# A two-layer hybrid mixer block: narrow matmuls grouped by shape, and the order of all instructions made anew

## The chip, the cores and the metric

The kernel runs on one core of a Trainium2 chip. Its metric is the device time of one execution in microseconds (us), from which the median of several executions is taken. Five engines work side by side, each through its own queue in order: TensorE (PE in the profile; its weight loads are PEld), VectorE (DVE), ScalarE (ACT), GpSimd (POOL) and SyncE (SP), which issues the DMAs here.

## The reference

Two layers over a stream x (512 tokens, 1024 channels), and in the first layer also over a context stream (256 tokens). Each layer scales and shifts the stream by vectors made from a condition (the modulation), projects it, mixes it in four ways, projects back, and applies a gated feed-forward block, with a layer norm after each half. Cut to what the change touches:

```python
def modulation(cond, w, b):                   # for two conditions, 6 x 1024 columns
    m = (jax.nn.silu(cond) @ w + b)[..., None, :]
    return jnp.split(m, 6, axis=-1)

# rwkv_prep, both directions d: two low-rank products (LoRA) of 64 columns each
logw  = -jax.nn.softplus(-(w0[d] + jnp.tanh(dw) @ w2[d])) - 0.5
decay = jnp.exp(-jnp.exp(logw)); a = jax.nn.sigmoid(a0[d] + da @ a2[d])

def step(S, inp):                             # rwkv_scan: token after token, 4 heads of 64
    s_kk = jnp.einsum('bhvk,bhk->bhv', S, -kk_t)
    S = S * w_t + s_kk[..., None] * (kk_t * a_t) + v_t[..., None] * k_t
    return S, jnp.einsum('bhvk,bhk->bhv', S, r_t)
```

The context is scanned first and hands its states to x. The other mixers (pooling, a gated MLP over chunks of 128 tokens, a Fourier mixer) and the feed-forward block are dense work beside the scan.

## The kernel before

Most of the arithmetic is dense: the projections and the feed-forward block multiply in three passes of fp32r (`mm3`: high by high, high by low, low by high), with 128 rows and 128 columns of the array in use and 512 or 256 tokens moving. Weights come as raw tiles of 128x1024 (512 KB, three buffers); ACT rounds them to a high part and DVE subtracts to get the low part (`wsplit`).

Between these stand matmuls that fill only a part of the array:

- `mod` (L671) makes two of the six modulation vectors. For each of 8 blocks of rows and each of two vectors it loads one raw tile and runs two matmuls of 32 columns and 512 moving elements (`ps<-raw,sc`). A raw tile fills two of the four groups of 32 columns, the next tile the other two. There are 5 such calls, 80 raw tiles in all; the first modulation is made in `start` in another layout, which already uses all four column groups with 256 elements.
- `group` (L1088) prepares 4 chunks of 64 tokens for one pair of heads, in both directions, and is called 12 times. It makes the LoRA products, the high part on 128 rows (`lh`), the low part on the 64 rows of its direction (`ll`); then, for each head, four matmuls with weights from `BK` on 64 rows, and four transposes of `BK` on 64 rows.
- `inverse` (L1188), once a group, inverts eight triangular 64x64 blocks. The diagonal blocks of 16 are solved by substitution on DVE: 15 shuffles of rows (`NR<-Nc`), then 15 pairs of a product (`Rt`) and a sum (`Rc`). Blocks of 32 and 64 follow from matmuls of 32x32 in two stages, 96 of them.
- `scan` (L1248) takes four steps. A step has four or five places where both directions d of both heads e each need one small matmul: 64 columns on 128 rows (`ps<-page` 64x64), or 64 on 64 (`ps<-rhs,page`). The heads lie in different halves of the array's columns.

The code does not issue instructions in the order in which it is written. `Program` keeps each as an `Op` with an estimated cost; `latest` gives it a latest start, `LEAD` (L255) moves each labelled part by a number of nanoseconds, and `schedule` (L353) places instructions one by one by that priority, if buffers suffice. A TensorE instruction of another kind than the last costs `SWITCH` there, and kinds are only fp32r or not. Each matmul is its own `Op`, so that the three of an `mm3` or the four of a scan place can be torn apart. Scans run beside dense work: `main` merges the two parts with `both`.

Of the kernel before, what the change touches and what calls it, by code (L numbers as in the profile page):

```python
# [32 lines left out]
# packed constants  # L33
C_B64 = 0
C_MG = 128
C_M0, C_E0, C_E1, C_D16 = 640, 704, 736, 768
C_SCAN = 784
C_EDGE = 1040
C_RW = 1072
C_N = 1074  # L40
# [7 lines left out]
P_N = 72  # L48

# [3 lines left out]
def part(f):  # L53
    """A method whose instructions are moved together in time."""

    def g(self, *a, **k):
        p = self.nc
        up, p.lab = p.lab, (*p.lab, f.__name__, *(getattr(x, "name", x) for x in a if isinstance(x, (int, Stream))))
        r = f(self, *a, **k)
        p.lab = up  # L60
        return r

    return g


class Op:
    """One instruction, held back until its place is known."""

    def __init__(self, i, eng, meth, args, kw, lab):
        self.i, self.eng, self.meth, self.args, self.kw, self.lab = i, eng, meth, args, kw, lab  # L70
# [4 lines left out]
        self.outs, self.ins = outs, ins  # L75
        self.dma = meth == "dma_start"
        self.table = ACT_SET.get(kw.get("func")) if eng == "scalar" else None
        self.price()

    def price(self):  # L80
        """Estimated time on its engine and until others see its result, in ns."""
        size = lambda a: math.prod(c for _, c in list(a.ap)[1:])
        n, k = size(self.outs[0]), self.kw
        ps = any(a.space == PSUM for a in self.outs + self.ins)
        ptr = sum(isinstance(k.get(x), bass.AP) for x in ("scale", "bias", "scalar1", "scalar2", "scalar"))
        if self.dma:
            self.cost, self.bytes = 60.0, 4 * n * self.outs[0].partition_size()
        elif self.eng == "tensor":
            w = self.args[1]
            m, kp = size(w), w.partition_size()  # L90
            self.table = 1 + (w.dtype == F32R)
            self.cols = n * kp / 128 * (1 if w.dtype == F32R else 2 if self.meth == "transpose" else 4)
            if w.dtype == F32R:
                self.cost = (n if n >= 256 else 4 * max(n, m)) / 2.4 + 2.5
            elif self.meth == "transpose":
                self.cost = 2 * kp / 2.4 + 2.5
            elif m > 64:
                self.cost = 4 * max(n, m) / 2.4 + 5
            else:
                self.cost = n / 1.2 + 30 if m > 32 else n / 2.4 + 26 if kp > 32 else 35.0  # L100
        elif self.eng == "vector":
            if self.meth in ("tensor_reduce", "bn_stats"):
                n = size(self.ins[0])
            elif self.meth == "bn_aggr":
                n = 8
            elif self.meth == "reciprocal":
                n *= 6
            elif self.meth in ("tensor_copy", "tensor_scalar", "memset") and not ps:
                n /= 2
            self.cost = 69 + n / 0.96 + 61 * ptr  # L110
        elif self.eng == "scalar":
            self.cost = (51 if ps else 93) + n / 1.2 + 93 * ptr
        elif k.get("op") == ALU.pow:
            self.cost = 300 + 165 * n
        else:
            self.cost = 110 + n * {"tensor_tensor": 2.24, "tensor_copy": 3.4, "tensor_scalar": 5.6}.get(self.meth, 1)


class Program:
    """Takes the place of nc: keeps the instructions of the kernel as a list."""  # L120
# [8 lines left out]
    def __init__(self, nc):  # L129
        self.nc, self.ops, self.lab = nc, [], ()  # L130
        for e in ENGINES:
            setattr(self, e, Program.Engine(self, e))

    def add(self, eng, meth, args, kw):
        self.ops.append(Op(len(self.ops), eng, meth, args, kw, self.lab))

    def both(self, a, b):
        """Two independent parts, merged by their progress."""
# [16 lines left out]
class Tiles:  # L155
    """Stands in for the tile pools: gives tiles their memory when their first instruction is placed."""
# [36 lines left out]
def region(a, cache={}):  # L193
    """Partitions and the set of free elements (as bits) that an access covers."""
# [13 lines left out]
def analyse(ops):  # L208
    """What each instruction has to come after, and the tiles it touches.

    A matmul that starts a sum also acts on the other sums in the same rows of its bank."""
    live = {}
    for o in ops:
        o.preds, o.succ, o.tiles = set(), [], []
        new = []
        for w, aps in ((True, o.outs), (False, o.ins)):
            for a in aps:
                nm = a.name
                if a.space == DRAM:
                    if not nm.startswith("keep"):  # L220
                        continue
                    p0, p1, m = 0, 1, 1
                else:
                    if nm not in o.tiles:
                        o.tiles.append(nm)
                    p0, p1, m = region(a)
                acc = o.kw.get("start") if w and o.eng == "tensor" else None
                for j, jw, q0, q1, jm, je, jacc in live.get(nm, ()):
                    if j in o.preds or (not w and not jw and not (a.space == PSUM and je != o.eng)):
                        continue  # L230
                    if (a.space == PSUM and je != o.eng) or (p0 < q1 and q0 < p1 and (
# [1507 lines left out]
```

## Time and profile before

| | |
|---|---|
| time, median of 3 runs | 1966.04 us (1961.61 to 1971.19) |
| span of the profiled execution, first to last instruction | 1969.1 us |
| PE busy | 1851.2 us, 94% of the span |
| PE weight loads busy | 1399.8 us, 71% |
| DVE busy | 1330.0 us, 68% |
| ACT, POOL busy | 728.1 us, 589.6 us (37%, 30%) |
| moved by DMA | 233.56 MB, 119 GB/s over the span |

The profiled execution has no time of its own beside its span; the span lies inside the range of the three timed runs. An fp32 matmul leaves two records in the profile, an fp32r matmul or a transpose one, so that x8 in a row of `ps<-page 128x64` is four matmuls. A record's end is modelled and reaches into the next, so rows of neighbours overlap. Nearly all instructions carry line L491, the line that emits them; they are told apart by the names of their tiles.

### The profile page before, as it was taken

How to read it: one execution, taken by the hardware profiler on the slowest of the kernel's cores; microseconds unless marked ns; L12 is line 12 of the kernel's file. 1: busy time of each engine (PE TensorE's matmuls, PEld its weight loads, DVE VectorE, ACT ScalarE, POOL GpSimd, SP SyncE). 2: the span in 40 equal slices, each digit the busy share in tenths (PEclk: the TensorE clock that was granted, in tenths of full speed). 3: DMA queues.
4: the chain of work that ended last, by engine and by line, in shares of the span. 5: the costliest groups of instructions: out<-in, count | busy, mean ns of one | idle time of the engine just before them, and what ended most of it. 6: DMA issues, size and time to landing. Idle time of an engine off the chain costs nothing. (4 is left out here: it accounts for less than half of the span.)

```text
span 1969.1 us, 32607 instructions
## 1 busy us (share of the span) xinstructions
PE 1851.2 (94%) x12400; PEld 1399.8 (71%) x12400; DVE 1330.0 (68%) x3047; ACT 728.1 (37%) x1445; POOL 589.6 (30%) x651
## 2 busy tenths in 40 slices
PE   7999899899989999899999999999989999999996
PEld 4886655587867668778777777767545677788875
DVE  3596968887998688734745478786895953443446
ACT  2573643444643334422322232544432232222220
POOL 3132443331342334600112114222553361100015
PEclk9998899899999999999999998988889999999998
DMA  8532147453534651333222232211454323323241
GB/s 295 182 109 80 65 153 224 149 166 130 176 125 155 199 170 59 106 97 97 86 93 79 83 100 92 81 55 31 135 182 153 113 83 94 97 86 107 86 128 43
DMA packets 86221, 233.56 MB, mean 119 GB/s; under 512 B 9008, under 2 KB 10416, under 8 KB 86064
## 3 DMA queue, kind: packets, MB, share of 16 engines
q1 hardware_dynamic: 86064, 231.48, 36.5%
q8 instruction: 97, 1.59, 0.3%
q14 instruction: 60, 0.49, 0.1%
HBM read 225.15 MB, written 6.29 MB: 118 GB/s over the span
## 5 line engine op out<-in xcount | busy, mean ns | idle before, releaser
L491 PE MATMUL ps<-page,w 128*128 128x512 f32 (+1 forms) x4512 | 957.5, 362 | 40.1 <-DVE w L491 26.4
L491 PEld LDWEIGHTS ps<-page,w 128*128 128x128 f32 x4512 | 742.2, 193 | 199.6 <-DVE w L491 45.2
L491 DVE TENSOR_TENSOR w<-raw,w 128x512 fp32r<-128x512 f32 (+1 forms) x526 | 407.2, 791 | 387.6 <-PE ps L491 312.6
L491 POOL TENSOR_TENSOR page<-page 128x512 f32<-128x512 f32 (+6 forms) x266 | 345.2, 1308 | 765.7 <-DVE page L491 616.1
L491 ACT ACTIVATE w<-raw 128x512 fp32r<-128x512 f32 (+1 forms) x526 | 314.5, 624 | 590.4 <-PE ps L491 458.3
L491 PE MATMUL ps<-w,page 128*128 128x512 f32 (+1 forms) x1704 | 413.2, 380 | 10.6 <-DVE w L491 6.0
L491 PEld LDWEIGHTS ps<-w,page 128*128 128x128 f32 x1704 | 295.0, 190 | 81.1 <-DVE w L491 10.4
L491 PE MATMUL ps<-page 128*64 128x64 f32 (+1 forms) x1832 | 219.2, 284 | 8.0 <-DVE page L491 3.7
L491 PEld LDWEIGHTS ps<-page 128*64 128x64 f32 (+1 forms) x1832 | 157.2, 157 | 87.1 <-issue 29.1
L491 ACT ACTIVATE page<-ps 128x512 f32<-128x512 f32 (+5 forms) x271 | 109.8, 421 | 218.9 <-PE ps L491 210.4
L491 DVE TENSOR_TENSOR page<-ps,page 128x512 f32<-128x512 f32 x210 | 143.0, 684 | 52.7 <-PE ps L491 42.4
L491 PE MATMUL ps<-raw,sc 128*32 128x512 f32 (+1 forms) x448 | 106.3, 574 | 12.8 <-DMA raw<-in_w_mod_dram 6.4
L491 POOL TENSOR_TENSOR page<-half,page 128x256 fp32r<-128x256 f32 (+2 forms) x72 | 61.1, 852 | 163.3 <-DVE page L491 107.2
L491 POOL TENSOR_TENSOR Sd<-page,pc 64x128 f32<-64x128 f32 x88 | 44.7, 508 | 154.1 <-DVE page L491 139.6
L491 ACT ACT_TABLE_LOAD x58 | 74.4, 1283 | 10.9 <-DVE half L491 7.1
L491 DVE TENSOR_TENSOR page<-ps,cst 64x256 f32<-64x256 f32 (+1 forms) x136 | 66.7, 498 | 13.3 <-PE ps L491 11.0
L491 POOL TENSOR_TENSOR page<-page,half 64x256 f32<-64x256 f32 (+1 forms) x54 | 45.8, 849 | 97.6 <-DVE half L491 52.4
L491 DVE TENSOR_TENSOR Rt<-Rc,NR 128x16 f32<-128x16 f32 (+4 forms) x180 | 73.6, 409 | 1.4
L491 DVE STREAM_SHUFFLE NR<-Nc 128x120 f32<-128x120 f32 (+4 forms) x180 | 67.6, 560 | 0.0
L491 PE MATMUL ps<-idn,page 128*128 128x128 f32 (+1 forms) x276 | 53.6, 305 | 6.9 <-ACT page L491 2.4
L491 DVE SCALAR_TENSOR_TENSOR page<-ps,pc,Sd 64x64 f32<-64x64 f32 x176 | 43.4, 280 | 21.4 <-PE ps L491 19.0
L491 PEld LDWEIGHTS ps<-page,BK 64*128 64x128 f32 x384 | 42.8, 198 | 18.5 <-issue 12.9
(123 smaller groups left out, 1439.7 us busy)
## 6 DMA issues: line engine op xcount, KB each, us to landing
raw<-in_w_dram SPq DMA_DIRECT2D x196, 512.0 KB, 3.7
raw<-in_w_mod_dram SPq DMA_DIRECT2D x80, 512.0 KB, 4.2
raw<-in_win_dram SPq DMA_DIRECT2D x45, 512.0 KB, 3.3
raw<-in_w_out_dram SPq DMA_DIRECT2D x24, 512.0 KB, 4.4
raw<-in_wm_dram SPq DMA_DIRECT2D x16, 512.0 KB, 4.2
page<-in_rows_dram SPq DMA_DIRECT2D x23, 256.0 KB, 4.8
page<-in_x_dram SPq DMA_DIRECT2D x16, 256.0 KB, 5.7
raw<-in_wk_dram SPq DMA_DIRECT2D x8, 384.0 KB, 3.4
```

What stands on the lines that cost most here:

```text
L491: r = getattr(getattr(nc, o.eng), o.meth)(*[conv(x) for x in o.args], **{k: conv(x) for k, x in o.kw.items()})
```

## The change

Six things change together.

1. `mod` has its weights laid out so that a raw tile holds 256 columns of four quarters. A tile now feeds four matmuls of 256 elements, one in each column group. The bytes and the number of tiles stay.
2. The low part of the LoRA weights is padded with zeros to 128 rows, so `ll` runs on full rows.
3. `inverse` starts from diagonal blocks of 8: 7 shuffles and 7 pairs on DVE in place of 15, and one more stage of 64 matmuls of 32x32, with a transpose and two elementwise steps.
4. In `group` the matmuls of both heads, and then the transposes of both, alternate between the heads.
5. `one()` makes a single `Op` of several TensorE instructions: an `mm3`, four matmuls of a scan place, eight of `group`, a stage of `inverse`, four of `mod`.
6. The costs know six shapes of the array and a higher `SWITCH`; `LEAD` and `RULES` have new numbers, and the order of everything follows from them.

```diff
+    def one(self):
+        up, self.together = self.together, self.together or Op(0, "tensor", self.lab)
+        yield
+        self.together = up
...
-            self.table = 1 + (w.dtype == F32R)
...
+        r, c = (next(32 << q for q in range(3) if x <= 32 << q) for x in (kp, m))
+        self.table = table = 2 if r == c == 128 else 3 + r // 64 * 3 + c // 64
...
-SWITCH = {"scalar": 1283.0, "tensor": 55.0}
+SWITCH = {"scalar": 1283.0, "tensor": 130.0}
...
-    12810, -15656, -33268, -28192, 10280, -19873, 190053, 102494, -5177, 56613, 240624, 225391, 88602, 53603, 75696,
...
+    15854, -25100, -27221, 21355, 10347, -6600, 290736, -111429, -14390, -242951, 894440, 296459, 37815, 112936,
...
-        for k in range(NK):
-            for z, v in enumerate(vs):
-                w = self.wload([(lambda r: r, self.I["w_mod"][l, k * 128:(k + 1) * 128, v * 1024:(v + 1) * 1024])])
-                for j in range(2):
-                    o = 64 * z + 32 * j
-                    self.mm(ps[o:o + 32, :], self.sc32[:, k, :], w[:, j * 512:(j + 1) * 512], k == 0, k == NK - 1)
+        for h in range(2):
+            c = slice(h * 256, h * 256 + 256)
+            for k in range(NK):
+                w = self.wload([(lambda r: r, self.I["wm"][l, MODS.index(vs), h, k])])
+                with nc.one():
+                    for q in range(4):
+                        self.mm(ps[32 * q:32 * q + 32, c], self.sc32[:, k, :], w[:, q * 256:(q + 1) * 256],
+                                k == 0, k == NK - 1)
...
-                self.mm(ps[:, z * 256:z * 256 + 256], ll[rd, z, o], st.lr[z][d][rd, sl], False, True)
+                self.mm(ps[:, z * 256:z * 256 + 256], ll[:, z, d, o], st.lr[z][d][:, sl], False, True)
...
+            with nc.one():
+                for j in range(4):
+                    for e in range(2):
+                        self.mm(pgs[e][:, j * 128 + qs[e]:j * 128 + qs[e] + nq], bk(e, j),
+                                AR[d][e][own[e], j, qs[e]:qs[e] + nq])
...
-        for s in range(15):
-            V.stream_shuffle(out=NR[:, :, s:15, s + 1], in_=Nc[:, :, s + 1:16], mask=[i // 16 * 16 + s for i in range(32)])
+        for s in range(7):
+            V.stream_shuffle(out=NR[:, :, s:7, s + 1], in_=Nc[:, :, s + 1:8], mask=[i // 8 * 8 + s for i in range(32)])
...
-        for t_ in range(1, 16):
+        for t_ in range(1, 8):
...
+        for mask in (self.ea, self.eb):
+            Rb, Tb, Y, R32 = R32, self.half([128, 8, 32]), self.half([128, 8, 32]), self.half([128, 8, 32])
+            V.transpose(out=Tb, in_=Rb)
...
-            for d, e in both:
-                self.mm(ps[e][own[e], c0 + d * 64:c0 + d * 64 + 64], AR[d][e][:, j, own[e]], W[e][:, j, d, :], d == 0,
-                        False, **kw)
+            with nc.one():
+                for d, e in both:
+                    self.mm(ps[e][own[e], c0 + d * 64:c0 + d * 64 + 64], AR[d][e][:, j, own[e]], W[e][:, j, d, :], d == 0,
+                            False, **kw)
```

What this does to TensorE's order shows at two places. The first is the first calls of `group`, on the context of layer 0. Before, in TensorE's queue (`BK` rows are `group`, the others dense work and the Fourier mixer):

```order
L491 MATMUL ps<-page,BK 128x128 x4
L491 MATMUL ps<-w,page 128x256 x10
L491 MATMUL ps<-page,w 128x256
L491 MATMUL ps<-half,bd 128x256
L491 MATMUL ps<-page,w 128x256 x22
L491 MATMUL ps<-w,page 128x256 x2
L491 MATMUL ps<-page,w 128x256 x3
L491 MATMUL ps<-page,BK 128x128 x4
```

The same place now:

```order
L547 MATMUL ps<-page,BK 128x128 x8
L547 MATMUL ps<-page,w 128x256 x24
L547 MATMUL ps<-half,bd 128x256 x2
L547 MATMUL ps<-w,page 128x256 x12
L547 MATMUL ps<-page,w 128x256 x12
L547 MATMUL ps<-w,page 128x256 x12
L547 MATMUL ps<-page,BK 128x128 x8
```

The four matmuls of one head and the four of the other no longer stand apart; each eight is one direction of both heads, and dense matmuls come in threes.

The second place is the end of the modulation of layer 1, beside the last scans of x. Before, in TensorE's queue (`raw,sc` is `mod`, `half` is `inverse`, 64x64 is `scan`):

```order
L491 MATMUL ps<-half,page 32x32 x16
L491 MATMUL ps<-page 64x64 x2
L491 MATMUL ps<-rhs,page 64x64 x2
L491 MATMUL ps<-page 64x64 x2
L491 MATMUL ps<-raw,sc_111 32x512 x2
L491 MATMUL ps<-rhs,page 64x64 x2
L491 MATMUL ps<-page 64x64
L491 MATMUL ps<-half 32x32 x16
L491 MATMUL ps<-page 64x64 x4
L491 MATMUL ps<-raw,sc_111 32x512
```

The same place now:

```order
L547 MATMUL ps<-half,page 32x32 x32
L547 MATMUL ps<-page 64x64 x8
L547 MATMUL ps<-raw,sc_122 32x256 x4
L547 MATMUL ps<-rhs,page 64x64 x4
L547 MATMUL ps<-raw,sc_122 32x256 x4
L547 MATMUL ps<-half 32x32 x32
L547 MATMUL ps<-page 64x64 x8
L547 MATMUL ps<-page,sp 128x512
L547 MATMUL ps<-w,page 128x256 x6
```

Places of two matmuls, or of one, have become places of four or eight. Counted over the whole queue, the shape of the array changes 939 times from one matmul to the next before and 625 times now, and the number of runs of dense matmuls between such changes falls from 353 to 251.

## Rows read from the trace of the kernel before

**Rows 1.** The page's busy times and shares, by engine.

```profile
PE 1851.2 (94%) x12400; PEld 1399.8 (71%) x12400; DVE 1330.0 (68%) x3047; ACT 728.1 (37%) x1445; POOL 589.6 (30%) x651
```

**Rows 2.** Windows, two stretches with scans: PE, PEld, DVE, ACT, POOL; clock, DMA, GB/s.

```profile
0.00:770.00 770.00, 711.44 (x5713) 535.50 (x5713) 600.72 (x1484) 351.97 (x714) 264.24 (x334) 0.97 0.48 155
1240.00:1560.00 320.00, 301.44 (x2480) 198.46 (x2478) 253.89 (x700) 128.55 (x282) 120.85 (x131) 0.92 0.35 109
```

**Rows 3.** Waits of PE: us in total, times, longest.

```profile
PE ps L491 <- DVE page L491: 18.4, 27, 3.8
```

**Rows 4.** Groups by form on PE: xrecords, busy us, mean ns, idle before.

```profile
L491 PE MATMUL ps<-page,w 128*128 128x256 f32 x1800 | 262.0, 296 | 17.5 <-DVE w L491 8.6 <-DVE page L491 4.7 <-DVE half L491 2.7
L491 PE MATMUL ps<-page 128*64 128x64 f32 x1376 | 101.8, 246 | 6.7 <-DVE page L491 3.2 <-DVE half L491 2.9 <-ACT page L491 0.4
L491 PE MATMUL ps<-raw,sc 128*32 128x512 f32 x320 | 95.0, 631 | 6.4 <-DMA raw<-in_w_mod_dram 6.4
...
L491 PE MATMUL ps<-rhs,page 64*64 64x64 f32 x384 | 43.5, 240 | 1.8 <-DVE page L491 1.5
L491 PE MATMUL ps<-page,BK 64*128 64x128 f32 x320 | 40.3, 301 | 4.8 <-DVE BK L491 2.6 <-DVE Rc L491 2.2
...
L491 PE MATMUL ps<-idn,BK 64*128 64x64 f32 x192 | 21.3, 242 | 1.3 <-ACT page L491 1.0 <-DVE page L491 0.2
L491 PE MATMUL ps<-page,ll 64*128 64x256 f32 x48 | 19.4, 403 | 0.0
L491 PE MATMUL ps<-half 32*32 32x32 f32 x1152 | 18.7, 197 | 2.1 <-DVE half L491 2.0
L491 PE MATMUL ps<-half,page 32*32 32x32 f32 x1152 | 18.0, 196 | 7.1 <-DVE Rc L491 3.8 <-ACT page L491 2.0 <-DVE half L491 1.2
L491 PE MATMUL ps<-page,lh 128*128 128x256 f32 x48 | 17.4, 363 | 0.2 <-DVE page L491 0.2
```

**Rows 5.** Timeline of PE: start, length in us; one raw tile, in `start` and in `mod`.

```profile
22.80 0.64 PE L491 MATMUL ps<-raw,sc 128*32 128x256 f32 x8
...
363.30 1.05 PE L491 MATMUL ps<-raw,sc 128*32 128x512 f32 x4
```

**Rows 6.** Raw tiles from 1380 to 1520 us: min/median/max ns, first and last start.

```profile
L491 PE MATMUL ps<-raw,sc x128: 592/617/1062, 1381.2 to 1509.1; 128*32 128x512 f32 x128
```

**Rows 7.** The page's DMA rate in 40 equal slices, GB/s.

```profile
GB/s 295 182 109 80 65 153 224 149 166 130 176 125 155 199 170 59 106 97 97 86 93 79 83 100 92 81 55 31 135 182 153 113 83 94 97 86 107 86 128 43
```

**Rows 8.** Timeline of PE, places of the scan with two, four and eight matmuls.

```profile
186.69 0.75 PE L491 MATMUL ps<-page 128*64 128x64 f32 x16
187.36 0.50 PE L491 MATMUL ps<-page,w 128*128 128x512 f32 x1
...
190.06 0.45 PE L491 MATMUL ps<-page 128*64 128x64 f32 x4
...
196.52 0.45 PE L491 MATMUL ps<-page 128*64 128x64 f32 x8
...
283.59 0.46 PE L491 MATMUL ps<-rhs,page 64*64 64x64 f32 x8
```

**Rows 9.** Timeline of PE, matmuls and transposes of `BK` in `group`.

```profile
126.05 1.16 PE L491 MATMUL ps<-page,BK 64*128 64x128 f32 x8
...
313.37 0.47 PE L491 MATMUL ps<-idn,BK 64*128 64x64 f32 x8
...
608.75 1.72 PE L491 MATMUL ps<-page,BK 64*128 64x128 f32 x20
```

**Rows 10.** Timeline of PE, one stage of 32 matmuls in `inverse`.

```profile
169.17 0.75 PE L491 MATMUL ps<-half 32*32 32x32 f32 x64
```

**Rows 11.** Groups on DVE, the substitution in `inverse`: xcount, busy us, mean ns.

```profile
L491 DVE TENSOR_TENSOR Rt<-Rc,NR 128x16 f32<-128x16 f32 (+4 forms) x180 | 73.6, 409 | 1.4
L491 DVE STREAM_SHUFFLE NR<-Nc 128x120 f32<-128x120 f32 (+4 forms) x180 | 67.6, 560 | 0.0
L491 DVE TENSOR_REDUCE Rc<-Rt 128x8 f32<-128x16 f32 (+4 forms) x180 | 48.8, 271 | 1.4
```

More of the change, by code (lines that the diff above doesn't have):

```diff
@@ L130, in __init__ @@
         self.nc, self.ops, self.lab = nc, [], ()
+        self.together = None
         for e in ENGINES:
@@ L215, in analyse @@
         new = []
[L216 to L231, printed above, removed]
-                            m & jm or None not in (acc, jacc) and acc != jacc)):
-                        o.preds.add(j)
-                new.append((nm, (o.i, w, p0, p1, m, o.eng, acc)))
+        for w, a, acc in o.access:
+            nm = a.name
+            if a.space == DRAM:
+                if not nm.startswith("keep"):
+                    continue
+                p0, p1, m = 0, 1, 1
+            else:
+                if nm not in o.tiles:
+                    o.tiles.append(nm)
+                p0, p1, m = region(a)
+            for j, jw, q0, q1, jm, je, jacc in live.get(nm, ()):
+                if j in o.preds or (not w and not jw and not (a.space == PSUM and je != o.eng)):
+                    continue
+                if (a.space == PSUM and je != o.eng) or (p0 < q1 and q0 < p1 and (
+                        m & jm or None not in (acc, jacc) and acc != jacc)):
+                    o.preds.add(j)
+            new.append((nm, (o.i, w, p0, p1, m, o.eng, acc)))
         for nm, x in new:
@@ L392, in fits @@
                 b = front
-                if f > b and load[tg][b:f].max() + 1 > caps[tg]:
+                if f > b and load[tg][b:f].max() + new[tg] > caps[tg]:
                     return False
@@ L944, in w_in_v @@
             ps = self.psum()
-            for i in range(st.nt):
+            with nc.one():
+              for i in range(st.nt):
                 for e in range(2):
@@ L1179, in group @@
         for d in range(2):
-            for j in range(4):
+            with nc.one():
+              for j in range(4):
                 src = v[:, i * 256 + j * 64:i * 256 + j * 64 + 64] if d == 0 else vr[:, j * 64:j * 64 + 64]
@@ L1234, in inverse @@
         w = [q3(ps[:, 0:256]), q3(ps[:, 256:512])]
-        for q in range(8):
+        with nc.one():
+          for q in range(8):
             for e in range(2):
@@ L1239, in inverse @@
         V.tensor_copy(Y[b[1]], w[0][b[1]])
-        for q in range(8):
+        with nc.one():
+          for q in range(8):
             for e in range(2):
@@ L1275, in scan @@
                     self.tt(Sd[o], W[e][o, j], pc[o, :, j:j + 1].to_broadcast([64, 2, 64]), ALU.mult, nc.gpsimd)
-            for d, e in both:
+            with nc.one():
+              for d, e in both:
                 o = own[e]
@@ L1337, in readout @@
         z = self.tn(st)
-        for c in range(nch):
+        with nc.one():
+          for c in range(nch):
             nc.tensor.transpose(ps[c // 4][own[0], c % 4 * 128:c % 4 * 128 + 128], y[:, c, :], self.ident)
```

295 lines of the change are left out of this document (175 added, 120 removed), and 43 rows, old and new, of the table LEAD.

## The prediction

> **What bounds the kernel now.** I read the page's busy times first: PE is busy for 1851.2 us of a span of 1969.1, 94%, and no other engine is over 68% [rows 1]. A busy share can hide stages with another limit, so the windows came next: in the two stretches with scans, 0 to 770 and 1240 to 1560 us, PE is busy for 711.4 and 301.4 us, 92% and 94%, and DVE for 78% and 79% [rows 2]. The reader should see there that PE leads everywhere, with DVE not far behind. PE stands idle for 118 us in all. Its waits are short: the one for DVE's pages comes to 18.4 us in 27 times, 0.68 us each [rows 3]. So what PE no longer has to do is time saved, as long as nothing close behind takes its place. The groups by form then show what PE spends on narrow matmuls [rows 4], and the timeline what one place costs [rows 5, 8 to 10]. All terms are in busy time, as a row's length; a row overlaps the next, and that is corrected at the end.
>
> **Modulation.** 80 raw tiles take 95.0 us, 320 records at four a tile, 1.19 us each [rows 4]; undisturbed, one tile is 1.05 us [rows 5]. The new form is in the trace already: `start` runs four matmuls of 256 elements in four column groups, eight records in 0.64 us [rows 5]. 80 x 0.64 = 51.2, a gain of 44 us. Loads keep their number and bytes, on the same queue of SP. But where tiles now follow each other quickly the transfer is late next. The best rate of any slice is 295 GB/s [rows 7], so a tile of 512 KB (524 thousand bytes) needs 1.78 us and the last 32 tiles at least 57 us. They are spread over 128 us before [rows 6]. In the new order I count between the first and the last of them 32 places of `mod`, 25 of the scan, 6 stages of `inverse`, 7 places of `BK`, 42 dense matmuls of 256 and some 50 small others: by the rows of each 45 to 50 us of PE work. So 7 to 12 us come back as waiting; I take 12, with bounds of 0 (other work moves in) and 25 (GB/s as in the slices around, below 200).
>
> **LoRA on full rows.** `lh` and `ll` are 48 each and take 17.4 + 19.4 = 36.8 us; a dense matmul of the same 256 elements takes 262.0 / 1800 = 0.146 us [rows 4]. 96 x 0.146 = 14.0, a gain of 23 us. The zeros cost POOL four memsets, once a layer.
>
> **Units of both heads, scan.** Here the timeline tells most: four records (two matmuls) take 0.45 us, eight records (four matmuls) also 0.45, sixteen 0.75 [rows 8]. Two matmuls of one head lie in the same half of the columns; the other head's ride along in the other half. The new order has 57 runs of four, 50 of eight, 3 of sixteen and one of twelve: 57 x 0.45 + 50 x 0.75 + 60 x 0.094 = 69 us against 101.8 [rows 4], a gain of 33. The 64x64 form becomes 48 runs of four at 0.46 [rows 8]: 22 against 43.5 [rows 4], a gain of 21.
>
> **Units of both heads, group.** Four matmuls of one head take 1.16 us; a row of 20 records, ten matmuls with both heads mixed in, takes 1.72, which is 0.17 a matmul against 0.29 [rows 9]. If the heads fully overlap on their halves of the rows, each of 20 units of eight takes 1.16: 23 us against 40.3 [rows 4], a gain of 17. If not at all, 20 x 2 x 1.1 = 44, no gain. The transposes go from 21.3 us [rows 4] to 24 units of eight at 0.47 [rows 9], 11 us, a gain of 10 (bound: none). I take both gains, 27, since the mixed rows lie near them.
>
> **Inverse.** 24 stages more, 32 matmuls each; one takes 0.75 us [rows 10], so 18 us more on PE. The two old forms stay at 18.7 + 18.0 us. By the Trainium skill (TensorE: Matmul & The Clock Gate, Part 1) matmuls don't start closer than about 25 ns to each other; with two records a matmul that would make 24 x 64 x 25 ns = 38 us, and the sum would be 20 us less good. This trace disagrees: 64 records in 0.75 us are 12 ns apart. On DVE the three groups of the substitution come to 73.6 + 67.6 + 48.8 = 190 us for 15 steps [rows 11]; 8 of 15 go, 101 us. Three added instructions a call, at 0.56 us, the longest mean of these rows, are 20 us. DVE loses some 81 us, 7 us in each chain from `BK` to the scan. None of it is on PE, so it counts only where PE waits for DVE: between 0 and 18 us [rows 3], I take 8.
>
> **Order.** The array's shape changes 314 times less. Every such edge is counted in two rows: the row of 0.75 us at 186.69 reaches 0.08 us into the next [rows 8]. So 314 x 0.08 = 25 us of the gains above were never spent twice and go back. On the other side the dense runs that end at an edge fall by 102. No row prices what a dense run loses there alone; 0.08 us is the nearest row, and with a weight load that cannot be brought ahead I take twice that, 16 us (bounds 8 and 25). That an `mm3` stays together changes the number of dense matmuls not at all.
>
> **The sum.** -44 - 23 - 54 - 27 + 18 = -130; + 25 - 16 = -121 on PE; + 12 for transfers and - 8 for waits on DVE: -117. The profiled span of 1969 becomes 1852. The timed median lies 3 us below that span, so 1849.
>
> **The rivals.** One: PE's gain is partly not to be had, because the chain of small steps through DVE and ACT sets the pace in the stretches with scans, and PE's idle time there doubles. It is 58.6 + 18.6 = 77 us now [rows 2], so 1849 + 77 = 1926. For it: DVE at 78 and 79%, and fewer dense matmuls to fill with. Against it: DVE itself loses 81 us, and PE's waits are short now. The Trainium skill says so too (TensorEngine Tiling, PSUM Bottleneck): packing the array speeds up TensorE, not the emptying of PSUM, which may become the limit; rows 2 leave room, since DVE's and ACT's shares stay under PE's. Two: the heads don't overlap in `group` and the transfers take their upper bound: + 27 + 13, 1889. Three, slower: a unit starts only when the operands of both heads are there, and PE's queue is in order, so dense matmuls behind it wait as well, and then DVE and ACT, which wait for PE. There are 220 scan places and 48 of `group`. If each waits as long as one wait for DVE does now, 0.68 us [rows 3], that is 182 us, and the time 1849 + 182 = 2031. It decides from 117 / 268 = 0.44 us a unit on. For it: the halves of `rhs` are copied by two engines, and the later one counts. Against it: dense runs stand between most places in the new order, so operands have time. Four: half clock. PE's granted clock is 0.97 and 0.92 in the two stretches [rows 2]; where `mod` and narrow places stand without dense work it may fall. Were it 0.70 over the 60 us of the last tiles, half of 0.3 x 60 and more would be lost, 10 to 20 us: inside the range.
>
> **How the numbers follow.** The forecast 0.77, rival one 0.10, two 0.07, three 0.06. The forecast's own range: all upper bounds together (no transfer wait, 18 from DVE, 25 at dense ends) give 1849 - 12 - 10 - 9 = 1818, and the correction of 25 may be too large, 1795 with it; the lower ones (half of 27 lost, 13 for transfers, 8 at the ends, 8 for DVE, the clock 15) give about 1906. With most of rival two inside, the range is 1795 to 1910. Half a per cent is 10 us, about what a measurement of this kernel can tell from no change. Rival one ends at 2% faster, with a tail at no change: faster 0.91, same 0.03, slower 0.06.
>
> **What would show it.** In the new profile: `raw,sc` at about 51 us; `ll` and `lh` near 14 together; the scan's two forms near 69 and 22; `BK` eights of sixteen records at 1.2 us and not 2; 32x32 at 55 in all; DVE near 1250; PE near 1730 busy. Rows of PE waiting for raw tiles of `mod` late in layer 1 should add up to 7 to 25 us. It is wrong if PE's idle time grows well beyond 130 us, or if PE's busy time falls by less than 90.

## The result: 1888 us, and the profile after

The median of four executions is 1888.05 us (1885.32 to 1892.97); the kernel before, run beside it, gave 1967.72 (1961.61 to 1971.19). The ratio is 0.9592 with a 95% interval of [0.9556, 0.9628]: about 80 us less, where 117 were forecast. The time lies inside the predicted range and 39 us above the predicted value.

The page's busy times, as in [rows 1]:

```profile
span 1888.2 us, 35946 instructions
PE 1727.4 (91%) x14256; PEld 1365.5 (72%) x14256; DVE 1237.5 (66%) x2699; ACT 720.0 (38%) x1443; POOL 596.2 (32%) x655
```

PE is busy 123.8 us less (forecast 121) and DVE 92.5 us less (forecast 81). But the span fell by 80.9 only. So PE stands idle for 160.8 us now, against 117.9 before: 43 us of the shorter work came back as waiting. Which waits, the view of PE's waits says (us in total, times, longest). Before, with the row of [rows 3] as their second:

```profile
PE ps L491 <- DVE w L491: 32.5, 41, 2.6
...
PE ps L491 <- DVE half L491: 9.4, 9, 2.9
PE ps L491 <- ACT page L491: 6.9, 10, 2.0
PE ps L491 <- DMA raw<-in_w_mod_dram: 6.4, 8, 1.5
PE ps L491 <- DMA raw<-in_wm_dram: 6.2, 2, 4.7
PE ps L491 <- DVE Rc L491: 6.0, 2, 3.8
```

and after:

```profile
PE ps L547 <- DMA raw<-in_wm_dram: 35.1, 30, 5.5
PE ps L547 <- DVE w L547: 25.1, 31, 3.0
PE ps L547 <- DVE page L547: 20.9, 24, 2.7
PE ps L547 <- DVE half L547: 17.9, 16, 4.2
PE ps L547 <- ACT page L547: 14.8, 14, 2.7
PE ps L547 <- issue: 7.7, 6, 3.1
```

Waits for raw tiles of the modulation went from 12.6 to 35.1 us, in 30 pieces. Those for DVE stayed: 66.3 before in four rows, 63.9 in the three here and 4.3 more for `rhs`, although DVE does 92.5 us less. Those for ACT's pages doubled. Another 7.7 us are idle time for which the profile shows no cause (`issue`). Nothing shows one large stall.

Where it happens, the windows say (window, its length, PE, PEld, DVE, ACT, POOL busy; clock, DMA share, GB/s). The kernel before and then the changed one; the same window holds slightly later work in the second:

```profile
50.00:280.00 230.00, 216.97 (x1733) 167.88 (x1733) 176.22 (x460) 124.75 (x254) 76.65 (x90) 0.94 0.35 112
...
1300.00:1450.00 150.00, 141.97 (x1200) 89.50 (x1198) 118.58 (x356) 59.00 (x132) 61.92 (x72) 0.85 0.28 87
```

```profile
50.00:280.00 230.00, 202.27 (x2029) 163.57 (x2020) 163.24 (x406) 128.17 (x264) 76.38 (x90) 0.93 0.37 116
...
1300.00:1450.00 150.00, 114.71 (x1942) 78.25 (x1938) 114.05 (x341) 56.82 (x131) 74.42 (x73) 0.84 0.52 168
```

Length less PE busy is PE's idle time: from 13 to 28 us in the first, from 8 to 35 in the second. In all the windows up to 750 us and from 1300 to 1450 it is 64.6 before and 125.7 now; elsewhere it fell from 53 to 35. The growth sits where `group`, `inverse` and `scan` run. The granted clock is not the reason: 0.94 and 0.93, 0.85 and 0.84 in these two windows, 0.963 over the whole run in both kernels. In the second stretch DMA moves 168 GB/s in place of 87, since the last 32 tiles of the modulation now stand there within 87 us (1335 to 1422) and were spread over 128 before [rows 6]. The chain of waits shows it (start, length, what ended last):

```profile
1371.95 3.52 DMA raw<-in_wm_dram
1375.51 0.68 PE ps L547 x8
1376.21 4.52 DMA raw<-in_wm_dram
1380.78 1.12 PE ps L547 x8
1381.92 4.46 DMA raw<-in_wm_dram
1386.42 4.54 PE ps L547 x92
```

A tile lands, PE works 0.7 to 4.5 us, and waits for the next; 24.5% of the chain from 1300 to 1420 us is these transfers.

The groups by form answer to [rows 4] and [rows 10] (xrecords, busy us, mean ns, idle before):

```profile
L547 PE MATMUL ps<-page,w 128*128 128x512 f32 x2712 | 678.2, 401 | 7.9 <-DVE w L547 4.3 <-ACT page L547 2.9 <-POOL page L547 0.4
...
L547 PE MATMUL ps<-page 128*64 128x64 f32 x1376 | 72.3, 237 | 12.0 <-DVE page L547 9.0 <-ACT page L547 2.7
L547 PE MATMUL ps<-raw,sc 128*32 128x256 f32 x768 | 67.3, 432 | 37.5 <-DMA raw<-in_wm_dram 35.1 <-ACT half L547 2.0
...
L547 PE MATMUL ps<-half 32*32 32x32 f32 x1920 | 28.7, 198 | 11.8 <-DVE half L547 8.8 <-issue 3.0
L547 PE MATMUL ps<-half,page 32*32 32x32 f32 x1920 | 28.5, 198 | 16.0 <-DVE half L547 9.1 <-issue 4.7 <-ACT page L547 2.1
L547 PE MATMUL ps<-page,BK 64*128 64x128 f32 x320 | 26.0, 297 | 1.8 <-ACT half L547 1.6 <-DVE page L547 0.2
L547 PE MATMUL ps<-rhs,page 64*64 64x64 f32 x384 | 23.2, 238 | 5.0 <-DVE rhs L547 4.3 <-ACT rhs L547 0.7
L547 PE MATMUL ps<-page,lh 128*128 128x256 f32 x48 | 14.6, 322 | 5.6 <-ACT page L547 4.4 <-POOL page L547 1.2
L547 PE MATMUL ps<-page,ll 128*128 128x256 f32 x48 | 13.4, 298 | 0.0
```

The reader should see two things. The narrow forms fell about as forecast. And the places that begin a link of the scan's chain, the two 32x32 forms, wait: 27.8 us here, 9.2 in [rows 4]. Of the 27.8, DVE's halves ended 17.9, and for 7.7 the profile shows no cause.

### The profile page after: what moved, and what is told of

The parts are those of the page before. It is cut to its first block, busy times and chain, and to the rows that moved or that the text cites. A ratio compares the mean times of both kernels' runs of the same rounds, so it can differ in the third digit from the quotient of the medians.

```text
span 1888.2 us, 35946 instructions
## 1 busy us (share of the span) xinstructions
PE 1727.4 (91%) x14256; PEld 1365.5 (72%) x14256; DVE 1237.5 (66%) x2699; ACT 720.0 (38%) x1443; POOL 596.2 (32%) x655
## 4 chain that ended last, share of the span: by engine, by line
PE 55%; DVE 12%; DMA 5%; issue 3%; ACT 2%; POOL 1%; POOLq 0%; SPq 0%; ACTq 0%; DVEq 0%
PE ps L547 55%; DVE page L547 6%; DMA raw<-in_w_dram 3%; DVE w L547 3%; DMA raw<-in_wm_dram 2%; POOL page L547 1%; DVE half L547 1%; ACT w L547 1%; ACT page L547 1%; DVE s L547 1%; DVE NR L547 0%; DVE Nc L547 0%; ACT L547 0%; POOL rs L547 0%; DMA raw<-in_w_out_dram 0%
## 5 line engine op out<-in xcount | busy, mean ns | idle before, releaser
L547 PE MATMUL ps<-page,w 128*128 128x512 f32 (+1 forms) x4512 | 926.2, 358 | 31.7 <-DVE w L547 17.3
L547 POOL TENSOR_TENSOR page<-page 128x512 f32<-128x512 f32 (+5 forms) x266 | 347.8, 1319 | 740.4 <-DVE page L547 593.5
L547 PE MATMUL ps<-w,page 128*128 128x512 f32 (+1 forms) x1704 | 401.1, 382 | 11.2 <-DVE w L547 7.9
L547 PE MATMUL ps<-page 128*64 128x64 f32 (+1 forms) x1832 | 184.6, 277 | 12.3 <-DVE page L547 9.4
L547 PEld LDWEIGHTS ps<-page 128*64 128x64 f32 (+1 forms) x1832 | 137.9, 153 | 70.6 <-issue 25.4
L547 PE MATMUL ps<-raw,sc 128*32 128x256 f32 x768 | 67.3, 432 | 37.5 <-DMA raw<-in_wm_dram 35.1
L547 ACT ACT_TABLE_LOAD x56 | 71.8, 1283 | 20.0 <-PE ps L547 14.5
L547 PEld LDWEIGHTS ps<-raw,sc 128*32 128x32 f32 x768 | 16.7, 115 | 64.2 <-DMA raw<-in_wm_dram 48.5
L547 ACT ACTIVATE half<-ps,mcb,mcs 128x256 f32<-128x256 f32 x64 | 31.8, 564 | 62.3 <-PE ps L547 62.2
L547 DVE CAST page<-page 128x512 fp32r<-128x512 f32 (+1 forms) x86 | 44.7, 526 | 15.3 <-ACT page L547 6.7
L547 DVE SCALAR_TENSOR_TENSOR page<-ps,pc,Sd 64x64 f32<-64x64 f32 x176 | 42.5, 280 | 17.9 <-PE ps L547 11.0
```

Source lines behind the costliest of these rows:

```text
L547: r = getattr(getattr(nc, o.eng), meth)(*[conv(x) for x in args], **{k: conv(x) for k, x in kw.items()})
```

## The experiments

All but one keep the order of the changed kernel, or of the kernel before where that is said, so that each measures its edit and not a new order. The ratio is to the kernel before on the same chip; idle is the profiled span less PE busy. The changed kernel and the kernel before stand first. Only the intervals of mod_two_groups, subst_twice and all_eased lie apart from that of the changed kernel; for the others the difference in time is little more than a hint, and what counts is whether the rows and waits of the trace go with it.

| | time, us | ratio | PE busy | PE idle |
|---|---|---|---|---|
| before | 1967.72 | 1 | 1851.2 | 117.9 |
| changed | 1888.05 | 0.9592 [0.9556, 0.9628] | 1727.4 | 160.8 |
| half_mod | 1875.45 | 0.9543 [0.9512, 0.9574] | 1727.6 | 146.7 |
| raw4 | 1878.18 | 0.9554 [0.9521, 0.9586] | 1728.2 | 150.4 |
| mod_two_groups | 1904.34 | 0.9687 [0.9657, 0.9717] | 1752.9 | 151.6 |
| subst_twice | 1947.16 | 0.9907 [0.9877, 0.9936] | 1746.6 | 197.9 |
| subst_less | 1880.54 | 0.9549 [0.9487, 0.9610] | 1728.0 | 151.4 |
| bk_by_head | 1891.95 | 0.9614 [0.9564, 0.9665] | 1735.9 | 154.8 |
| scan_by_head | 1890.21 | 0.9612 [0.9560, 0.9663] | 1732.1 | 155.6 |
| lora_half_rows | 1896.80 | 0.9643 [0.9589, 0.9697] | 1746.0 | 154.3 |
| before_subst_less | 1952.91 | 0.9948 [0.9911, 0.9985] | 1832.6 | 113.8 |
| raw4_w | 1870.17 | 0.9540 [0.9487, 0.9592] | 1725.4 | 142.5 |
| old_lead, one run | 2201.60 | | 1850.9 | 348.6 |
| all_eased | 1859.14 | 0.9460 [0.9426, 0.9493] | 1720.6 | 134.9 |

**Half the bytes of each raw tile.**

```diff
+            if ins[0].name == "in_wm_dram":
+                self.bytes *= 2
...
-                w = self.wload([(lambda r: r, self.I["wm"][l, MODS.index(vs), h, k])])
+                w = self.wload([(lambda r: r[:, 0:512], self.I["wm"][l, MODS.index(vs), h, k][:, 0:512])])
...
-                        self.mm(ps[32 * q:32 * q + 32, c], self.sc32[:, k, :], w[:, q * 256:(q + 1) * 256],
+                        self.mm(ps[32 * q:32 * q + 32, c], self.sc32[:, k, :], w[:, q % 2 * 256:(q % 2 + 1) * 256],
```

> The order is that of the changed kernel, instruction for instruction, and PE's matmuls of the modulation are the same in number and size; only half of each raw tile of mod is loaded (256 KB in place of 512), and its four matmuls read that half twice, so half of the modulation's weights are left out. Theory (PE waits for transfers): the 35.1 us in which PE waits for raw tiles of wm fall below 15, and the time falls from 1888 by 15 to 25 us. Rival (chain of DVE and ACT beside it sets the pace): the waits only change their name to DVE half and DVE page, and the time falls by less than 6 us.

The time fell by 12.6 us, between the two outcomes, and the wait for raw tiles by 20.3, from 35.1 to 14.8 us. The difference is in the waits for DVE's halves and pages, 5.0 and 2.5 us longer than in the changed kernel.

**A fourth raw buffer.**

```diff
-        return Tiles.Pool(self, self.ctx.enter_context(self.tc.tile_pool(name=name, bufs=bufs, **kw)), bufs, kw.get("space"))
+        return Tiles.Pool(self, self.ctx.enter_context(self.tc.tile_pool(name=name, bufs=bufs + (1 if name == "raw" else 0), **kw)), bufs, kw.get("space"))
```

> Same order, all bytes loaded, but the pool of raw tiles has four buffers of 4 KB in place of three, so that a load can start one tile earlier. Theory (PE waits because a load can only start when one of three buffers is free, 4.4 us before it lands): waits for raw tiles of wm fall from 35.1 to about 15 to 20, those for w tiles a little, and the time falls by 10 to 20 us. Rival (bandwidth: the tiles follow each other as fast as the DMA engines move them): waits stay above 28, time within 5 us.

With all bytes loaded, one buffer more gives nearly the same, 9.9 us less (7.5 by the ratio; all its runs lie below all of the changed kernel's). PE's waits in it:

```profile
PE ps L547 <- DVE w L547: 28.7, 31, 3.1
PE ps L547 <- DVE page L547: 25.8, 31, 2.6
PE ps L547 <- DVE half L547: 19.4, 15, 4.0
PE ps L547 <- DMA raw<-in_wm_dram: 15.9, 9, 4.6
```

19.2 us of waiting for transfers went, and 10 us of it came back as waiting for DVE in the three rows above. So the late tiles were less a matter of bandwidth than of when a buffer came free for the next transfer, and what stood behind that wait was another.

**The modulation with two matmuls of 512 a tile again.**

```diff
...
-        for h in range(2):
-            c = slice(h * 256, h * 256 + 256)
-            for k in range(NK):
-                w = self.wload([(lambda r: r, self.I["wm"][l, MODS.index(vs), h, k])])
+        for k in range(NK):
+            for z, v in enumerate(vs):
+                w = self.wload([(lambda r: r, self.I["w_mod"][l, k * 128:(k + 1) * 128, v * 1024:(v + 1) * 1024])])
                 with nc.one():
-                    for q in range(4):
-                        self.mm(ps[32 * q:32 * q + 32, c], self.sc32[:, k, :], w[:, q * 256:(q + 1) * 256],
-                                k == 0, k == NK - 1)
+                    for j in range(2):
+                        o = 64 * z + 32 * j
+                        self.mm(ps[o:o + 32, :], self.sc32[:, k, :], w[:, j * 512:(j + 1) * 512], k == 0, k == NK - 1)
...
```

> Same order, but each raw tile of mod again feeds two matmuls of 512 elements in two column groups, as before the change (the layout of the weights with it). Theory (term of the sum, partly hidden under transfers): raw,sc grows from 67 us busy to about 105, waits for raw tiles fall from 35 to about 10 to 15, and the time grows by 12 to 28 us. Rival (PE bound everywhere, the term counts in full): plus 38 to 44 us.

The time rose by 16.3 us, while the rows of `raw,sc` rose by 30.3 (67.3 to 97.6, both forms) and PE busy by 25.5. Waits for these tiles fell from 35.1 to 26.7 us: a slower consumer waits less for the same transfers. So the new form is worth 16 us in this order, of the 32 that remain of the forecast's 44 after its 12 for transfers.

**The substitution twice.**

```diff
-        for q, (meth, args, kw) in enumerate(o.calls):
+        for q, (meth, args, kw) in enumerate(o.calls * (2 if again else 1)):
```

`again` holds for the shuffles, products and sums of `inverse`.

> Same order, but each of the 7 shuffles, 7 products and 7 sums of the substitution on blocks of 8 is issued twice on DVE (same result), which gives DVE some 85 us back and lengthens each chain from BK to the scan by about 7 us. Theory of the forecast (PE leads, DVE's relief is worth 8 us): plus 5 to 20 us. Rival (the chain through DVE sets the pace in the stretches with scans): plus 50 to 85 us.

59 us more, as the rival expected. The three DVE groups of the changed kernel answer to [rows 11] (xcount, busy us, mean ns):

```profile
L547 DVE TENSOR_TENSOR Rt<-Rc,NR 128x16 f32<-128x16 f32 (+6 forms) x84 | 22.7, 270 | 0.8
L547 DVE STREAM_SHUFFLE NR<-Nc 128x56 f32<-128x56 f32 (+6 forms) x84 | 19.5, 340 | 0.0
L547 DVE TENSOR_REDUCE Rc<-Rt 128x8 f32<-128x16 f32 (+6 forms) x84 | 16.9, 202 | 0.7
```

Their 59.1 us became 121.4 (41.5 + 46.8 + 33.1), and DVE's busy time rose by 60.2 us, from 1237.5 to 1297.7. No instruction of PE changed. Of the 56 us by which the profiled span grew, 37 are PE's idle time (160.8 to 197.9) and 19 are busy time of PE, for the same matmuls at a mean granted clock of 0.955 in place of 0.963. The waiting shows first of all for split weights, which share DVE's queue with the substitution:

```profile
PE ps L553 <- DVE w L553: 55.8, 40, 5.1
```

It was 25.1 us in the changed kernel. Read alone, this says that DVE's chain sets the pace once it is longer; the next two runs ask what a shorter one gives.

**Four of seven shuffles and products less.**

```diff
+            nc.ops[-1].skip = s >= 3
...
+            nc.ops[-1].skip = t_ >= 4
...
+            nc.ops[-1].calls[0][2]["in_"] = tm[:, :, 0:min(t_, 3) + 1]
```

An instruction marked `skip` keeps its place in the plan and isn't issued.

> The changed kernel, instruction for instruction in the same order, without the last four of the seven shuffles and the last four of the seven products of each call of inverse (the sums stay and add fewer columns); those steps of the substitution are left out of the result. That is 48 products and 48 shuffles less, about 13 + 11 = 24 us of DVE. Theory one (DVE's chain sets the pace in the stretches with scans, as doubling it gave back 59 of 60 us): the time falls by 15 to 24 us, to 1864 to 1873, and PE's waits for DVE halves and pages fall. Theory two (the step of the forecast, by which 81 us of DVE were worth 8): 2 to 3 us, 1885. Theory three (doubling hurt only because an order tuned for short steps cannot take longer ones; shorter ones give nothing back): 0 to 5 us, and dense work is simply placed where it was.

The rows of the three groups fell by 23.5 us (59.1 to 35.6), the time by 7.5. But rows of DVE overlap their neighbours, as PE's do, and DVE's busy time fell by 12.9 us only:

```profile
PE 1728.0 (92%) x14256; PEld 1364.9 (73%) x14256; DVE 1224.6 (65%) x2555; ACT 720.0 (38%) x1443; POOL 595.8 (32%) x655
```

The time lies between what theories one and three expected. Measured against the 12.9 us, more than half came back, where the rows say a third; but 7.5 us is near the scatter. PE's idle time fell by 9.4 us (160.8 to 151.4), and scan_by_head, in which hardly anything changes, lies 5 us lower as well. So 4 to 9 us of idle time for 13 of DVE stand beside 37 for 60 in the doubling: that shortening gives back less than lengthening costs isn't shown.

**The same in the kernel before**, 8 of 15 shuffles and products less:

```diff
+            nc.ops[-1].skip = s >= 7
...
+            nc.ops[-1].skip = t_ >= 8
...
+            nc.ops[-1].kw["in_"] = tm[:, :, 0:min(t_, 7) + 1]
```

> The kernel before, in its own order, without the last 8 of the 15 shuffles and the last 8 of the 15 products of each call of inverse (the sums stay and add at most 8 columns; those steps are left out of the result). About 75 us of DVE go, nothing of PE. It asks in the old order what the forecast priced at 8 us. Theory one (the forecast: PE hides the substitution): the time falls by 0 to 18 us. Theory two (relief is worth what it was worth when four steps were left out of the changed kernel, 7.5 of 24 us): by about 23 us. Theory three (it is worth its length, as in the doubling, 59 of 60): by 60 us or more.

The three DVE groups fell from the 190.0 us of [rows 11] to 114.1, but DVE's busy time only from 1330.0 to 1282.0:

```profile
PE 1832.6 (94%) x12400; PEld 1389.7 (71%) x12400; DVE 1282.0 (66%) x2759; ACT 728.1 (37%) x1445; POOL 589.8 (30%) x651
```

The time fell by 8.6 us, by the ratio's interval between 3 and 17, and PE's idle time by 4.1. (PE's busy time is 18.6 us lower in this profile though none of its instructions changed; the mean granted clock was 0.972 in place of 0.963.) Theory one holds: in the old order, with PE busy for 94%, 48 us of DVE's busy time are worth about the 8 us of the forecast. That is less than a fifth of it, where the doubling in the changed order cost 59 us for 60. Whether the order or the direction makes the difference isn't settled; the run before this one leans to the order.

**One head after the other in group.**

```diff
-                for j in range(4):
-                    for e in range(2):
+                for e in range(2):
+                    for j in range(4):
```

> The changed kernel in the same order; inside each unit of group the four matmuls of one head come before the four of the other, and so the transposes. Theory one (the heads lie in different halves of the rows and overlap when they alternate): a unit of BK goes from 1.09 to about 2.2 us and one of transposes from 0.39 to about 0.8, 20 x 1.1 + 24 x 0.4 = 32 us at most, of which 17 to 32 show in the time; BK 128x128 goes from 26.0 to 44 us or more. Theory two (nothing overlaps, and the gain came from runs of eight in place of four, so fewer changes of shape): within 5 us of the changed kernel, and the rows of BK stay at 26 and 11.

Between the theories on PE, and theory two in the time. The timeline of the changed kernel, and of this one (start, length, next row's start shows where it ends):

```profile
128.28 1.16 PE L547 MATMUL ps<-page,BK 64*128 64x128 f32 x16
129.37 1.93 PE L547 MATMUL ps<-page,w 128*128 128x256 f32 x14
```

```profile
128.74 1.71 PE L547 MATMUL ps<-page,BK 64*128 64x128 f32 x16
130.38 0.86 PE L547 MATMUL ps<-page,w 128*128 128x256 f32 x5
```

From start to next start eight matmuls take 1.09 us alternating and 1.64 head by head, not 2.2. Alternation is worth 0.55 us a unit, 10.5 us in the row (26.0 to 36.5), and the transposes 1.1. Of 8.5 us of PE busy about 4 show in the time, no more than the runs scatter.

**One head after the other in scan.**

```diff
-        both = [(d, e) for d in range(2) for e in range(2)]
+        both = [(d, e) for e in range(2) for d in range(2)]
```

> The changed kernel in the same order; the four matmuls of a scan place come as two of one head and two of the other, in place of alternating. Theory one (two matmuls in one half of the columns run one after the other, and the other head's are free only if they alternate): a place goes from 0.38 us, start to start, towards 0.6, and the time rises by 10 to 25 us. Theory two (the hardware overlaps the halves whatever the order within four): 64x64 rows stay at 72 and 23 us, the time within 5 us.

Theory two in the time, which can't be told from that of the changed kernel. A place of four matmuls stays; one of eight goes from 0.69 to 0.75 us of row length, and the first of the scan's two forms from 72.3 to 76.4 us.

**LoRA on half rows.**

```diff
+            if o.eng == "tensor" and args[1].name.startswith("ll"):
+                d = args[1].offset // 256 % 2
+                a[1:] = [x[d * 64:d * 64 + 64] for x in a[1:]]
```

> The changed kernel in the same order; the low part of the LoRA product runs on the 64 rows of its direction again, and its zeros are left unread. By the forecast, full rows were worth 23 us: then the time rises by about 20. By the rows of the two profiles they were worth 9 (lh and ll 36.8 before, 28.0 now): then it rises by 5 to 10. If the shape alone counts for nothing and the 9 came from the new neighbours: no change, and ll + lh stay at 28.

8.7 us more in time, which is the second case; PE's busy time rose by 18.6 us, which is nearer to the first. The timeline of one group in the changed kernel and here:

```profile
98.60 0.28 PE L547 MATMUL ps<-page,lh 128*128 128x256 f32 x1
98.72 0.28 PE L547 MATMUL ps<-page,ll 128*128 128x256 f32 x1
...
99.07 7.27 PE L547 MATMUL ps<-page,w 128*128 128x256 f32 x60
```

```profile
98.06 0.28 PE L551 MATMUL ps<-page,lh 128*128 128x256 f32 x1
98.27 0.38 PE L551 MATMUL ps<-page,ll 64*128 64x256 f32 x1
98.58 0.38 PE L551 MATMUL ps<-page,lh 128*128 128x256 f32 x1
...
99.21 7.36 PE L551 MATMUL ps<-page,w 128*128 128x256 f32 x60
```

From its first start to the start of the dense matmuls the group takes 0.47 us on full rows and 1.15 where full and half rows alternate. A start follows the last after 0.12 us in the first and 0.21 or 0.31 in the second, both at a granted clock of 1.00 (the upper level, 2.4 GHz): 0.1 to 0.2 us more beside each change of shape. The Trainium skill (TensorEngine Tiling (Array Packing), Key Properties) says that changing the mode, not merely the tile, drains the array; this trace agrees as far as it goes, for a stretch of half rows alone wasn't run. Summed over all 96 of these matmuls, from each start to the next less the idle time between, it is 29.2 us in the kernel before, 14.5 in the changed one and 29.8 here. So full rows are worth 15 us of PE, more than the 9 that the rows show.

**One more buffer for split weights, beside the fourth raw buffer.**

```diff
-        return Tiles.Pool(self, self.ctx.enter_context(self.tc.tile_pool(name=name, bufs=bufs, **kw)), bufs, kw.get("space"))
+        return Tiles.Pool(self, self.ctx.enter_context(self.tc.tile_pool(name=name, bufs=bufs + (1 if name in ("raw", "wp", "w") else 0), **kw)), bufs, kw.get("space"))
```

> The changed kernel in the same order with four buffers for raw tiles, and in the room that is left one more buffer for split weights. If the waits of PE for DVE's low parts (25 us in the changed kernel, 29 with four raw buffers) come from the split having no free buffer when DVE is idle: 5 to 15 us below four raw buffers alone, 1863 to 1873. If they come from DVE being behind: within 3 us of it, 1875 to 1881.

1870.17 us (1869.80 to 1876.24), 0.9540 of the kernel before. In absolute time 8 us below four raw buffers alone, by the ratio 3, since the kernel before was faster on this chip too (1961.52 us). The wait for split weights is 23.4 us against 28.7. The two theories aren't told apart. Of the versions that compute everything it has the lowest median: all its runs lie below all of the changed kernel's, though the intervals of the two ratios overlap.

**The changed instructions in the order that the old table gives.**

```diff
-    15854, -25100, -27221, 21355, 10347, -6600, 290736, -111429, -14390, -242951, 894440, 296459, 37815, 112936,
...
+    12810, -15656, -33268, -28192, 10280, -19873, 190053, 102494, -5177, 56613, 240624, 225391, 88602, 53603, 75696,
...
-RULES = {"horizon": 65099.2624, "sticky": {"scalar": 34223.6612, "tensor": 1280.6065}, "cold": 19745181862762.5}
+RULES = {"horizon": 81429.1534, "sticky": {"scalar": 34640.9461, "tensor": 1692.69775}, "cold": 35718399.9}
```

> The instructions of the changed kernel, placed with the table of numbers and the rules of the kernel before. If the order is what turns PE's shorter work into time, it is slower than the changed kernel by more than 50 us, with PE's busy time within 30 us of 1727 and the difference in PE's idle time. If the shapes and units alone carry the gain, it is within 30 us of 1888.

2201.6 us, one run. As expected much slower, with PE idle for 348.6 us, but PE's busy time was not near 1727: it was 1850.9. The same matmuls took 123 us more on PE, at a mean granted clock of 0.92 against 0.96. How much of that is the clock and how much shorter dense runs wasn't separated. The table is read off by position, one number for each labelled part, so its old numbers were never made for these instructions. What is shown is that the cheaper instructions carry no gain in an order that doesn't fit them; how much of the 80 us is shapes and how much order, this run can't say.

**Buffers, bytes and steps together.** The edits of raw4_w, half_mod and subst_less in one kernel.

> The changed kernel in the same order with one more raw buffer and one more buffer for split weights, half the bytes of each raw tile of mod, and without the last four shuffles and products of each call of inverse (half of modulation's weights and those steps of the substitution are left out of the result). Alone, the buffers, the bytes and the steps gave 10 to 13, 13 and 8 us; buffers and bytes ease the same wait. PE's idle time is 161 us in the changed kernel and 118 before. If late transfers and the steps on DVE are the whole growth, idle time falls to 115 to 125 us and the time to 1845 to 1853. If what is left is a chain that dense work no longer covers, idle time stays at 128 to 140 and the time at 1858 to 1868.

The time is 1859.14 us, idle 134.9: the second of the two outcomes. What PE waits for now:

```profile
PE ps L552 <- DVE w L552: 23.8, 29, 3.1
PE ps L552 <- DVE page L552: 22.2, 28, 2.7
PE ps L552 <- DVE half L552: 19.3, 10, 4.8
PE ps L552 <- ACT page L552: 11.8, 13, 3.0
PE ps L552 <- DMA raw<-in_wm_dram: 11.5, 9, 4.0
PE ps L552 <- issue: 7.4, 6, 2.7
```

Of 43 us by which idle time grew, 26 go with all three; 17 stay. The waits for raw tiles are back where they were (11.5 us, 12.6 before), and those for DVE are where they were all along: 69.3 us over all rows of the view, 68.8 in the changed kernel, 69.2 before. What stays above the kernel before is ACT, 20.7 us over all rows for 13.7, and the 7.4 us for which the profile shows no cause.

## Why the prediction was right, and where it was off

**PE's busy time** fell by 124 us for 121 forecast. That the total came so near is in part luck, since three sizes were off and cancelled. First, the narrow terms gave 102 us in their rows where 130 were taken. Most came near: modulation -39 for -44 (both forms of `raw,sc`, 106.3 to 67.3), scan -50 for -54 (145.3 to 95.5), group -14 for -17 and -10 for -10, inverse +20.5 for +18. LoRA gave -9 in its rows for -23: 0.146 us a matmul is a length without overlap, set against rows that overlap and count time twice. From start to start it gave 15; the two kinds of length must not be mixed in a difference. Second, the dense groups fell by 51 us for 16 (the largest alone by 21.8, 700.0 to 678.2), and small forms that the sum left out by 20. Third, what rows count twice: the forms on PE add up to 156.7 us more than its busy time before and 108.4 after, so 48 us go back where 25 were taken. DVE's -92.5 for -81 cancels too: the three groups fell by 130.9 us in their rows for 101, because the steps that went are the longer ones, the added steps take 15 for 20, and DVE's rows overlap.

**Transfers of the modulation.** Right in place and kind: late in layer 1, PE waits for raw tiles, 14.9 us between 1300 and 1450 in the 7 to 25 named, where the same tiles cost 0.6 before. But over the whole run it waits 22.5 us more than before, since the start and layer 0 wait longer too, 20.2 us for 12.0. Taken as +12; 10 to 13 us of time come back when the wait is eased.

**The step that failed in size: waits, on DVE and on what follows it.** The sum had PE's idle time grow by 4 us (+12 for transfers, -8 for DVE), and it grew by 43. By the view of waits, those for transfers took 26 us more over all rows, those for ACT 10.5, for POOL 1.5, and 7.7 have no cause in the profile; those for DVE gave back nothing (69.2 to 68.8). The -8 was a fair price in the old order, as the same relief showed there (8.6 us), though its bound of 18 rested on one of the four rows of waits for DVE, which come to 66.3. But the sum put it beside 121 us of shorter PE work, and in the changed order DVE's time seems to cost more: 59 us for 60 added, 7.5 for 13 taken away, the second near the scatter. Waits for ACT stood in the sum at nothing. The reading that fits is that PE, with less work before each place of `group`, `inverse` and `scan`, reaches it before the result that it needs; no run takes that link apart. Adding work to PE goes with it: in bk_by_head, lora_half_rows and mod_two_groups 52.6 us of PE busy cost 29 us of time, some 55% (the first two are hardly above the scatter), and the change as a whole converts 124 into 80, 65%.

**The rivals.** One was the nearest in mechanism: in its own windows of [rows 2] idle time went from 77 to 135 us, where a doubling would be 154. It was off in that the other stretches gained 15, and a part of the waiting was for transfers. The Trainium skill (TensorEngine Tiling (Array Packing), PSUM Bottleneck) says that packing speeds up TensorE but not the emptying of PSUM. The prediction let the busy shares overrule it, and the trace after bears it out: sorted by the step of DVE or ACT that ended them, PE's waits for steps that read PSUM went from 23.1 to 44.3 us, and those for other steps from 59.8 to 48.8. A share below PE's doesn't show room where the steps follow one another. Two has the right number by accident: the heads do overlap, and though the wait for transfers came near its upper bound (22.5 us of 25), only 10 to 13 of it show in the time. Three didn't come: the idle time before the scan's two forms and `BK` is 18.8 us against 13.3 in [rows 4]. Dense matmuls stand between the places, as was argued. Four came in part: over the last 32 tiles the granted clock was 0.82 (1335 to 1422 us), 0.92 over the same tiles before (1381 to 1509), not 0.70. Over the whole run it was 0.963 both times, so it explains nothing of the miss.

**What stays open.** Put back one at a time in the changed order, the old form of the modulation, half rows in LoRA and one head after the other in `group` and `scan` cost 16, 9, 4 and 2 us, 31 of the 80. The rest wasn't separated: the units that `one()` makes, the shorter substitution with its added stage, and the order made anew, among them the 51 us of the dense rows. The last 17 us of idle time lie in waits for ACT and in idle time without a cause in the profile; which link is late wasn't isolated. The diff of the estimated costs holds more than the list of the change names (DVE and POOL take turns on a port there), and that shapes the order too. Nor was it tried what shorter steps are worth once the order is made anew for them.

## What to carry to other kernels

When an engine that is busy for 94% is given 7% less work, price the waits again at the new length and not at the old: here two thirds of the saving reached the time. Measure the price of another engine's work in the order in which it will stand: relief of DVE gave 8.6 us for 48 us of its busy time in the old order, and 60 us more cost 59 in the new one. Take such a price from the engine's busy time, not from rows, which overlap. After matmuls get denser in a stretch, look at how many buffers their loads have: one raw buffer more took 19 us of waiting away and was worth 8 to 10 us of time.

## What the runs showed of the hardware

Eight matmuls with weights of 64 rows take 1.09 us when they alternate between the two halves of the rows and 1.64 when they come in two fours; but four fp32 matmuls of 64 columns take the same in either order. Alternating an fp32r matmul of 256 elements on 128 rows with one on 64 costs 0.21 and 0.31 us from start to start, and 0.12 on equal rows: among matmuls on full rows, reading zeros is cheaper than using half of the array. Rows of DVE overlap as PE's do: without 16 of the substitution's steps a call, its three groups are 75.9 us shorter in their rows and the engine is busy for 48.0 us less.
